# Attention over short sequences: Q and K loaded in 8 KB runs, 32 heads a transfer, with chunks of every other head

## The chip, the cores and the metric

The kernel runs on one core of a Trainium2 chip. The metric is the device time of one execution in microseconds (us), a median over several runs. Profiles come from single executions; their span (first to last instruction) is some 1.8 us shorter than the time measured for the same run.

A core has a matrix engine (TensorE, PE in the profile), a vector engine (VectorE, DVE), a scalar engine (ScalarE, ACT), GpSimd (POOL), a sync engine (SP) and 16 transfer engines (DMA) between HBM and the core's memory (SBUF). Matmuls write to PSUM. Loads issued by GpSimd here also cast fp32 to bf16; their descriptors are made in software ("software_dynamic"). Stores are issued by ScalarE and SP ("hardware_dynamic", queues q10 and q1).

## The reference

```python
batch, n_heads, seq, head_dim = 32, 12, 128, 64       # q, k, v: fp32, randn * 0.1
scores = scale * np.matmul(q, k.transpose(0, 1, 3, 2))  # scale = 1 / sqrt(64)
scores_max = np.max(scores, axis=-1, keepdims=True)
attn = np.exp(scores - scores_max)
attn = attn / (np.sum(attn, axis=-1, keepdims=True) + 1e-8)
return np.matmul(attn, v).astype(np.float32)
```

There are 384 heads of 32 KB a tensor: 37.75 MB are read and 12.58 MB written.

## The kernel before

A chunk is 16 heads in a row, and there are 24. Each partition holds a run of 16 rows of one head (4 KB in HBM). For a chunk, VectorE turns Q and K in blocks of 32 x 32, TensorE computes scores (keys on partitions), ScalarE takes exp, TensorE makes the denominators and the outputs, VectorE turns those back, GpSimd multiplies by the reciprocals, and a store of 512 KB goes out. V comes in 12 blocks of 32 heads and is put in order by matmuls against a permutation ("values").

```python
def runs(x, t):
    return x.rearrange("b h (g t) d -> (b h g) (t d)", t=t).rearrange(
        "(n p) x -> p n x", p=128)

qr, kr, vr, orr = runs(q, TQ), runs(k, TQ), runs(v, T), runs(out, TQ)   # TQ = 16, T = 8

def load_qk(c):                                  # one chunk, 256 KB of bf16 each
    for src, which in ((qr, 0), (kr, 1)):
        x = pin.tile([128, TQ, D], bf16, ...)
        nc.gpsimd.dma_start(out=x, in_=src[:, c, :].rearrange("p (t d) -> p t d", t=TQ))
        chunks[c, which] = x

early = {0: 0, 1: 1, 2: 2, 3: 3, 4: 4, 5: 5}     # which V block is queued behind which chunk's Q and K
early.update({4 * m - 5 + i: 2 * m + i for m in range(3, NCH // 4) for i in range(2)})
# ... (turn, scores, values, denominators, outputs, divide, finish, scale_rows)

def store(c, eng):
    o_sb, _ = osbs.pop(c)
    eng.dma_start(out=orr[:, c, :], in_=o_sb.rearrange("p t d -> p (t d)"))

e = NCH - 1
held = {c: [c - LAG] if c >= LAG else [] for c in range(e - 3)}   # LAG = 9: stores wait nine chunks
held[e - 3] = [e - 12, e - 11, e - 10, e - 9]                     # and go out in bursts at the end
held[e - 2] = [e - 8, e - 7, e - 6]
held[e - 1] = [e - 5, e - 4, e - 3]
held[e] = [e - 2, e - 1, e]
for c in range(NCH):
    todo = shuffles.get(c, [])                   # V block pair c // 4 + 1 is put in order during chunk c
    if c < e:
        turn(c + 1, 0)
        turn(c + 1, 1)
    d_ps = denominators(c)
    if c < e:
        scores(c + 1)
    divide(c, d_ps)
    finish(c, 0, outputs(c, 0))
    # ... values(*x) for the first half of todo, finish(c, 1, outputs(c, 1)), values for the rest
    if c + AHEAD < NCH:                          # AHEAD = 7
        load(c + AHEAD)
    scale_rows(c)
    for s in held[c]:
        store(s, nc.scalar if s < e - 2 else nc.sync)
```

The softmax here doesn't subtract the row's maximum and nothing guards it: scores larger than these inputs give would overflow.

Of the kernel before, what the change touches and what calls it, by code (L numbers as in the profile page):

```python
# [10 lines left out]
def kernel(  # L11
# [8 lines left out]



    nc = tc.nc
    f32 = mybir.dt.float32
    bf16 = mybir.dt.bfloat16

    B, H, S, D = q.shape
    assert S == 128 and D == 64
    scale = 1.0 / (D ** 0.5)
    TQ = 16  # L30
    GQ = S // TQ
    T = 8
    A = 8
    CB = 4
    NCH = B * H // 16
    AHEAD = 7
    LAG = 9

    def runs(x, t):
        return x.rearrange("b h (g t) d -> (b h g) (t d)", t=t).rearrange(  # L40
            "(n p) x -> p n x", p=128)

    qr, kr, vr, orr = runs(q, TQ), runs(k, TQ), runs(v, T), runs(out, TQ)

    singles = ctx.enter_context(tc.tile_pool(name="singles", bufs=1))
    pin = ctx.enter_context(tc.tile_pool(name="pin", bufs=AHEAD + 3))
    pt = ctx.enter_context(tc.tile_pool(name="pt", bufs=3))
    pa = ctx.enter_context(tc.tile_pool(name="pa", bufs=3))
    pf = ctx.enter_context(tc.tile_pool(name="pf", bufs=8))
    po = ctx.enter_context(tc.tile_pool(name="po", bufs=LAG + 3))  # L50
    ps = ctx.enter_context(tc.tile_pool(name="ps", bufs=1, space=bass.MemoryType.PSUM))

    chunks, qts, attns, v2s, osbs = {}, {}, {}, {}, {}

    def load_qk(c):
        for src, which in ((qr, 0), (kr, 1)):
            x = pin.tile([128, TQ, D], bf16, tag="qk"[which] + "_bf", name="qk"[which] + "_bf")
            nc.gpsimd.dma_start(out=x, in_=src[:, c, :].rearrange("p (t d) -> p t d", t=TQ))  # L58
            chunks[c, which] = x

    def load_v(m):

        if m % 2 == 0:
            chunks[m // 2, 2] = pin.tile([128, 2 * CB, T, D], bf16, tag="v_bf", bufs=3, name="v_bf")
        nc.gpsimd.dma_start(  # L65
            out=chunks[m // 2, 2][:, m % 2 * CB:(m % 2 + 1) * CB],
            in_=vr[:, m * CB:(m + 1) * CB, :].rearrange("p n (t d) -> p n t d", t=T))

    with tc.manual_schedule():
        early = {0: 0, 1: 1, 2: 2, 3: 3, 4: 4, 5: 5}  # L70
        early.update({4 * m - 5 + i: 2 * m + i for m in range(3, NCH // 4) for i in range(2)})

        def load(c):
            load_qk(c)
            if c in early:
                load_v(early[c])

        for src, which, eng, cast in ((qr, 0, nc.sync, nc.vector.tensor_copy),
                                      (kr, 1, nc.scalar, nc.scalar.copy)):
            raw = po.tile([128, TQ, D], f32, tag="o_sb", name="raw")  # L80
            eng.dma_start(out=raw, in_=src[:, 0, :].rearrange("p (t d) -> p t d", t=TQ))
            x = pin.tile([128, TQ, D], bf16, tag="qk"[which] + "_bf", name="qk"[which] + "_bf")
            cast(x, raw)  # L83
            chunks[0, which] = x
        load_v(early[0])
        load_qk(1)
        ident = singles.tile([128, 128], bf16)
        make_identity(nc, ident)
        load_v(early[1])
        perm = singles.tile([128, A, 2, 32], bf16)  # L90
        nc.vector.memset(perm, 0.0)
        for tl in range(2):
            nc.vector.tensor_copy(
                perm[:, :, tl, tl * 16:(tl + 1) * 16].rearrange("p a (x g) -> p a x g", x=2),
                ident.rearrange("p (a g x) -> p a x g", a=A, x=2))
        ones = singles.tile([128, 32], bf16)
        nc.vector.memset(ones, 1.0)
        for c in range(2, AHEAD):
            load(c)

        def turn(c, which):


            x = chunks.pop((c, which)).bitcast(f32)
            xt = pt.tile([128, 4, S], f32, tag="qk"[which] + "t", name="qk"[which] + "t")
            if which == 0:
                nc.vector.transpose(xt.rearrange("p h (x g) -> p x h g", g=GQ), x)  # L107
            else:
                nc.vector.transpose(xt.rearrange("p h (x g) -> p x h g", g=GQ),  # L109
                                    x.rearrange("p (y t) e -> p t y e", y=2))  # L110
            qts[c, which] = xt.bitcast(bf16).rearrange("p h (s j) -> p h s j", j=2)

        def scores(c):
            qt, kt = qts.pop((c, 0)), qts.pop((c, 1))
            s_ps = ps.tile([128, 4, 4, S], f32, tag="s_ps", name="s_ps")
            for h in range(4):
                for j in range(2):
                    for b in range(4):
                        pr = slice(b * 32, (b + 1) * 32)
                        nc.tensor.matmul(  # L120
                            s_ps[:, b, h, :], lhsT=kt[pr, h, :, j], rhs=qt[pr, h, :, j],
                            start=(j == 0), stop=(j == 1), tile_position=(b * 32, 0))
            attn = pa.tile([128, 4, 4, S], bf16, tag="attn", name="attn")
            nc.scalar.activation(out=attn, in_=s_ps, func=mybir.ActivationFunctionType.Exp,  # L124
                                 bias=0.0, scale=scale)
            attns[c] = attn

        def values(m, a, heads, half):
# [16 lines left out]
        def denominators(c):  # L145

            d_ps = ps.tile([128, 4, S], f32, tag="w_ps", bufs=4, name="d_ps")
            for b in range(4):
                nc.tensor.matmul(  # L149
                    d_ps[b * 32:(b + 1) * 32], lhsT=ones, rhs=attns[c][:, b],  # L150
                    start=True, stop=True, tile_position=(0, b * 32))
            return d_ps

        def outputs(c, j):

            o_ps = ps.tile([128, 4, S], f32, tag="w_ps", bufs=4, name="o_ps")
            for h in range(4):
                for b in range(4):
                    nc.tensor.matmul(  # L159
                        o_ps[b * 32:(b + 1) * 32, h],  # L160
                        lhsT=v2s[c // 4][:, 4 * (b % 2) + h, 2 * (c % 4) + b // 2,
                                         j * 32:(j + 1) * 32],
                        rhs=attns[c][:, b, h], start=True, stop=True, tile_position=(0, b * 32))
            return o_ps
# [4 lines left out]
        def divide(c, d_ps):  # L169
            dt = pf.tile([128, TQ, 32], f32, tag="dt", name="dt")  # L170
            nc.vector.transpose(dt, turned(d_ps))  # L171
            recip = pf.tile([128, TQ], f32, tag="recip", name="recip")
            nc.vector.reciprocal(recip, dt[:, :, 0])  # L173
            osbs[c] = (po.tile([128, TQ, D], f32, tag="o_sb", name="o_sb"), recip)

        def finish(c, j, o_ps):
            o_sb, _ = osbs[c]
            nc.vector.transpose(o_sb[:, :, j * 32:(j + 1) * 32], turned(o_ps))  # L178

        def scale_rows(c):  # L180
            o_sb, recip = osbs[c]
            if c < NCH - 1:
                nc.gpsimd.tensor_mul(o_sb, o_sb, recip.to_broadcast([128, TQ, D]))  # L183
            else:
                for eng, sl in ((nc.gpsimd, slice(0, 32)), (nc.vector, slice(32, 64))):
                    eng.tensor_mul(o_sb[:, :, sl], o_sb[:, :, sl],  # L186
                                   recip.to_broadcast([128, TQ, 32]))

        def store(c, eng):
            o_sb, _ = osbs.pop(c)  # L190
            eng.dma_start(out=orr[:, c, :], in_=o_sb.rearrange("p t d -> p (t d)"))

        e = NCH - 1
        held = {c: [c - LAG] if c >= LAG else [] for c in range(e - 3)}
# [6 lines left out]
        for c in range(2):  # L201
            shuffles[c] = [(0, 4 * c + 2 * i, 2, 1) for i in range(2)]
            shuffles[c + 2] = [(1, 4 * c + i, 1, None) for i in range(4)]
        turn(0, 0)
        turn(0, 1)
        scores(0)
        for a in range(0, A, 2):
            values(0, a, 2, 0)
        for c in range(NCH):
            todo = shuffles.get(c, [])  # L210
            if c < e:
                turn(c + 1, 0)
                turn(c + 1, 1)
            d_ps = denominators(c)
            if c < e:
                scores(c + 1)
            divide(c, d_ps)
            finish(c, 0, outputs(c, 0))
            for x in todo[:len(todo) // 2]:
                values(*x)  # L220
            finish(c, 1, outputs(c, 1))
            for x in todo[len(todo) // 2:]:
                values(*x)
            if c + AHEAD < NCH:
                load(c + AHEAD)
            scale_rows(c)
            for s in held[c]:
                store(s, nc.scalar if s < e - 2 else nc.sync)
# [30 lines left out]
```

## Time and profile before

| | |
|---|---|
| time, median of 3 runs | 131.39 us (130.83 to 131.76) |
| span of the profiled run | 129.4 us |
| busiest engine | VectorE, 67% |
| transfer engines | at 9 tenths or more in 38 of 40 slices |
| last load lands, last compute ends, last store packet ends | 109.9, 122.5, 127.8 us |

The page's second section cuts the span into 40 slices, a digit for the tenths that an engine was busy. Section 3 has the transfer queues, section 4 the chain of waits followed back from the last instruction, section 5 the groups of instructions (count, busy us, mean ns, then the idle time before them and what ended it). The lines that carry the argument are in the prediction.

### The profile page before, as it was taken

The numbers are of one execution on the slowest core, as the hardware profiler recorded it, in microseconds if no ns is written. First come the engines' busy times: TensorE is split into PE (matmuls) and PEld (weight loads), VectorE is DVE, ScalarE is ACT, GpSimd is POOL, SyncE is SP. The second block draws the span as 40 slices with busy tenths as digits, with TensorE's granted clock in tenths as the row PEclk, the third lists the DMA queues.
The fourth block names the chain that finished last, engine by engine and source line by source line (L and its number), as shares of the span: only waits on it lengthen the run. The fifth ranks groups of instructions, "written<-read, shape, count | busy, mean of one in ns | idle before, by whom it ended". The sixth has DMA issues, their size and how long they took to land.

```text
span 129.4 us, 4637 instructions
## 1 busy us (share of the span) xinstructions
PE 72.9 (56%) x2080; PEld 43.6 (34%) x2080; DVE 86.5 (67%) x150; ACT 71.3 (55%) x74; POOL 79.5 (61%) x88
## 2 busy tenths in 40 slices
PE   0049537597746763886622976460977764856000
PEld 0037335334323442354402454220642442535000
DVE  0246576658879697879944589854578999795800
ACT  3219908567948745865760857580637777335000
POOL 6933133335799986998724895909999445553500
PEclk9999976869999999599996579998555999555555
DMA  3999999999999999999999999999999999999991
GB/s 114 275 193 205 209 209 208 208 210 205 211 208 212 204 211 209 209 208 210 282 288 281 208 212 282 288 286 246 250 209 286 236 298 317 405 414 399 412 408 54
DMA packets 16723, 32.27 MB, mean 249 GB/s; under 512 B 1344, under 2 KB 7488, under 8 KB 16704
## 3 DMA queue, kind: packets, MB, share of 16 engines
q0 software_dynamic: 12960, 18.35, 79.8%
q10 hardware_dynamic: 3168, 11.54, 23.0%
q1 hardware_dynamic: 576, 2.10, 4.2%
q8 instruction: 16, 0.26, 0.7%
q14 instruction: 3, 0.02, 0.0%
HBM read 37.75 MB, written 12.58 MB: 389 GB/s over the span
## 4 chain that ended last, share of the span: by engine, by line
DMA 56%; DVE 14%; POOL 11%; PE 9%; issue 2%; ACT 1%; POOLq 0%; DVEq 0%; ACTq 0%
DMA k_bf<-in_k_dram 34%; DMA q_bf<-in_q_dram 11%; DMA v_bf<-in_v_dram 11%; DVE o_sb L178 6%; PE s_ps L120 5%; POOL o_sb L183 4%; POOL v_bf L65 4%; DVE kt L109 3%; PE o_ps L159 3%; DVE qt L107 3%; POOL q_bf L58 2%; ACT attn L124 1%; PE v_ps L139 1%; DVE o_sb L186 1%; POOL k_bf L58 1%
## 5 line engine op out<-in xcount | busy, mean ns | idle before, releaser
L124 ACT ACTIVATE attn<-s_ps 128x2048 bf16<-128x2048 f32 x24 | 45.1, 1879 | 40.6 <-PE s_ps L120 38.5
L183 POOL TENSOR_TENSOR o_sb<-o_sb,recip 128x1024 f32<-128x1024 f32 x23 | 44.0, 1915 | 9.9 <-DVE o_sb L178 9.7
L178 DVE STREAM_TRANSPOSE o_sb<-o_ps 128x512 f32<-128x512 f32 x48 | 33.3, 712 | 15.7 <-PE o_ps L159 14.8
L120 PE MATMUL s_ps<-qt,kt 32*128 32x128 bf16 x768 | 18.6, 245 | 34.2 <-DVE kt L109 34.2
L139 PE MATMUL v_ps<-v_bf,perm 128*32 128x512 bf16 (+1 forms) x448 | 35.0, 418 | 2.7 <-DMA v_bf<-in_v_dram 2.0
L120 PEld LDWEIGHTS <-kt 32*128 32x128 bf16 x768 | 13.8, 106 | 44.2 <-DVE kt L109 44.2
L143 ACT CAST v<-v_ps 128x512 bf16<-128x512 f32 x48 | 26.1, 593 | 2.1 <-PE v_ps L139 2.0
L159 PE MATMUL o_ps<-attn,v 128*32 128x128 bf16 x768 | 22.9, 251 | 1.1 <-issue 1.0
L58 POOL DMA_DIRECT2D k_bf<-in_k_dram x23 | 12.3, 535 | 15.7 <-DMA v_bf<-in_v_dram 11.6
L109 DVE STREAM_TRANSPOSE kt<-k_bf 128x512 f32<-128x512 f32 x24 | 16.4, 684 | 6.2 <-DMA k_bf<-in_k_dram 6.1
L107 DVE STREAM_TRANSPOSE qt<-q_bf 128x512 f32<-128x512 f32 x24 | 16.3, 679 | 5.5 <-DMA q_bf<-in_q_dram 5.4
L159 PEld LDWEIGHTS <-v 128*32 128x32 bf16 x768 | 16.0, 111 | 10.3 <-issue 5.2
L65 POOL DMA_DIRECT2D v_bf<-in_v_dram x12 | 9.3, 778 | 13.0 <-DMA k_bf<-in_k_dram 4.2
L171 DVE STREAM_TRANSPOSE dt<-d_ps 128x512 f32<-128x512 f32 x24 | 16.3, 680 | 1.0 <-PE d_ps L149 1.0
L149 PE MATMUL d_ps<-attn,ones 128*32 128x512 bf16 x96 | 11.2, 453 | 9.0 <-ACT attn L124 8.9
L58 POOL DMA_DIRECT2D q_bf<-in_q_dram x23 | 13.2, 576 | 3.0 <-DMA k_bf<-in_k_dram 1.3
L139 PEld LDWEIGHTS <-perm 128*32 128x32 bf16 x448 | 11.8, 114 | 6.2 <-issue 3.5
L149 PEld LDWEIGHTS <-ones 128*32 128x32 bf16 x96 | 4.4, 103 | 15.4 <-issue 13.2
L173 DVE RECIPROCAL recip<-dt 128x16 f32<-128x16 f32 x24 | 6.1, 254 | 1.9
L83 DVE CAST q_bf<-raw 128x1024 bf16<-128x1024 f32 x1 | 0.7, 694 | 5.5 <-DMA raw<-in_q_dram 5.5
L83 ACT CAST k_bf<-raw 128x1024 bf16<-128x1024 f32 x1 | 1.0, 1045 | 3.2 <-DMA raw<-in_k_dram 3.2
L83 ACT ACT_TABLE_LOAD x1 | 1.3, 1283 | 1.2 <-PEq L243 1.2
(11 smaller groups left out, 3.9 us busy)
## 6 DMA issues: line engine op xcount, KB each, us to landing
out_dram<-o_sb ACTq DMA_DIRECT2D x21, 512.0 KB, 6.8
v_bf<-in_v_dram POOLq DMA_DIRECT2D x12, 512.0 KB, 13.5
q_bf<-in_q_dram POOLq DMA_DIRECT2D x23, 256.0 KB, 12.4
k_bf<-in_k_dram POOLq DMA_DIRECT2D x23, 256.0 KB, 12.4
out_dram<-o_sb SPq DMA_DIRECT2D x3, 512.0 KB, 6.4
raw<-in_k_dram ACTq DMA_DIRECT2D x1, 512.0 KB, 4.9
raw<-in_q_dram SPq DMA_DIRECT2D x1, 512.0 KB, 4.7
```

Source lines behind the costliest of these rows:

```text
L58: nc.gpsimd.dma_start(out=x, in_=src[:, c, :].rearrange("p (t d) -> p t d", t=TQ))
L107: nc.vector.transpose(xt.rearrange("p h (x g) -> p x h g", g=GQ), x)
L109: nc.vector.transpose(xt.rearrange("p h (x g) -> p x h g", g=GQ), x.rearrange("p (y t) e -> p t y e", y=2))
L120: nc.tensor.matmul(s_ps[:, b, h, :], lhsT=kt[pr, h, :, j], rhs=qt[pr, h, :, j], start=(j == 0), stop=(j == 1), tile_position=(b * 32, 0))
L124: nc.scalar.activation(out=attn, in_=s_ps, func=mybir.ActivationFunctionType.Exp, bias=0.0, scale=scale)
L139: nc.tensor.matmul(v_ps[u * 32:(u + 1) * 32, i], lhsT=perm[:, a + i, tl, :], rhs=v_bf[:, ns, 2 * u + tl, :], start=(tl == 0), stop=(tl == ...
L143: nc.scalar.copy(v2s[m][:, a:a + heads, ns], v_ps)
L149: nc.tensor.matmul(d_ps[b * 32:(b + 1) * 32], lhsT=ones, rhs=attns[c][:, b], start=True, stop=True, tile_position=(0, b * 32))
L159: nc.tensor.matmul(o_ps[b * 32:(b + 1) * 32, h], lhsT=v2s[c // 4][:, 4 * (b % 2) + h, 2 * (c % 4) + b // 2, j * 32:(j + 1) * 32], rhs=attn ...
L171: nc.vector.transpose(dt, turned(d_ps))
L178: nc.vector.transpose(o_sb[:, :, j * 32:(j + 1) * 32], turned(o_ps))
L183: nc.gpsimd.tensor_mul(o_sb, o_sb, recip.to_broadcast([128, TQ, D]))
```

## The change

The intent is longer runs in HBM: 8 KB for Q and K, in half as many transfers. Each partition then holds 32 rows of a head, and 128 partitions hold 32 heads (a duo of chunks). A turn handles all 32 heads, and a chunk takes every other one, so that its output still comes as runs of 16 rows (4 KB). On the HBM side a store is therefore 16 blocks of 8 rows ("16 x 8" or "blocked"): a row here is a run of 4 KB, a block is one head, and between two blocks lies a head of the other chunk. V blocks are queued at every even chunk.

```diff
-    AHEAD = 7
+    NDUO = NCH // 2
+    AHEAD = 5
-    qr, kr, vr, orr = runs(q, TQ), runs(k, TQ), runs(v, T), runs(out, TQ)
+    qr, kr, vr = runs(q, 2 * TQ), runs(k, 2 * TQ), runs(v, T)
+    orr = out.rearrange("b h s d -> (b h s d)").rearrange(
+        "(m k i p x) -> m i k p x", m=NDUO, k=16, i=2, p=8)
...
+    def load_qk(m, which):
+        x = pin.tile([128, 2 * TQ, D], bf16, tag="qk"[which] + "_bf", name="qk"[which] + "_bf")
+        nc.gpsimd.dma_start(
+            out=x, in_=(qr, kr)[which][:, m, :].rearrange("p (t d) -> p t d", d=D))
...
-            xt = pt.tile([128, 4, S], f32, tag="qk"[which] + "t", name="qk"[which] + "t")
+            xt = pt.tile([128, 8, S], f32, tag="qk"[which] + "t", name="qk"[which] + "t")
+            nc.vector.transpose(
+                xt.rearrange("p h (x g) -> p x h g", g=4),
+                x.rearrange("p (y t) e -> p t y e", t=(TQ, T)[which]))
...
-                            s_ps[:, b, h, :], lhsT=kt[pr, h, :, j], rhs=qt[pr, h, :, j],
+                            s_ps[:, b, h, :], lhsT=kt[pr, 2 * h + c % 2, :, j],
+                            rhs=qt[pr, 2 * h + c % 2, :, j],
...
-            nc.scalar.activation(out=attn, in_=s_ps, func=mybir.ActivationFunctionType.Exp,
-                                 bias=0.0, scale=scale)
+            nc.scalar.activation(
+                out=attn.rearrange("p b h (x g y) -> p (b h x) g y", g=4, y=2),
+                in_=s_ps.rearrange("p b h (x y g) -> p (b h x) g y", g=4, y=2),
+                func=mybir.ActivationFunctionType.Exp, bias=0.0, scale=scale)
...
-            eng.dma_start(out=orr[:, c, :], in_=o_sb.rearrange("p t d -> p (t d)"))
+            eng.dma_start(out=orr[c // 2, c % 2], in_=o_sb.rearrange("p t d -> p (t d)"))
...
-            if c < e:
-                turn(c + 1, 0)
-                turn(c + 1, 1)
+            if c < e - 1:
+                turn(c // 2 + 1, c % 2)
...
-            if c + AHEAD < NCH:
-                load(c + AHEAD)
+            if c % 2 == 0 and c // 2 + 6 < NDUO:
+                load_v(c // 2 + 6)
+            if c // 2 + AHEAD < NDUO:
+                load_qk(c // 2 + AHEAD, c % 2)
```

Cut: the buffer counts, the opening loads (1 MB transfers that stay fp32, "raw", for the first duo, cast by halves on VectorE and ScalarE; blocks 2 to 5 of V between the first Q and K), the permutation's pattern, and the head index in the outputs.

More of the change, by code (lines that the diff above doesn't have):

```diff
@@ L41, in runs @@
             "(n p) x -> p n x", p=128)
-    qr, kr, vr, orr = runs(q, TQ), runs(k, TQ), runs(v, T), runs(out, TQ)
+    qr, kr, vr = runs(q, 2 * TQ), runs(k, 2 * TQ), runs(v, T)
+    orr = out.rearrange("b h s d -> (b h s d)").rearrange(
+        "(m k i p x) -> m i k p x", m=NDUO, k=16, i=2, p=8)
     singles = ctx.enter_context(tc.tile_pool(name="singles", bufs=1))
-    pin = ctx.enter_context(tc.tile_pool(name="pin", bufs=AHEAD + 3))
-    pt = ctx.enter_context(tc.tile_pool(name="pt", bufs=3))
+    pin = ctx.enter_context(tc.tile_pool(name="pin", bufs=AHEAD))
+    pt = ctx.enter_context(tc.tile_pool(name="pt", bufs=2))
     pa = ctx.enter_context(tc.tile_pool(name="pa", bufs=3))
@@ L53 @@
     chunks, qts, attns, v2s, osbs = {}, {}, {}, {}, {}
-    def load_qk(c):
-        for src, which in ((qr, 0), (kr, 1)):
-            x = pin.tile([128, TQ, D], bf16, tag="qk"[which] + "_bf", name="qk"[which] + "_bf")
-            nc.gpsimd.dma_start(out=x, in_=src[:, c, :].rearrange("p (t d) -> p t d", t=TQ))
-            chunks[c, which] = x
+    def load_qk(m, which):
+        x = pin.tile([128, 2 * TQ, D], bf16, tag="qk"[which] + "_bf", name="qk"[which] + "_bf")
+        nc.gpsimd.dma_start(
+            out=x, in_=(qr, kr)[which][:, m, :].rearrange("p (t d) -> p t d", d=D))
+        chunks[m, which] = x
     def load_v(m):
@@ L69 @@
     with tc.manual_schedule():
-        early = {0: 0, 1: 1, 2: 2, 3: 3, 4: 4, 5: 5}
-        early.update({4 * m - 5 + i: 2 * m + i for m in range(3, NCH // 4) for i in range(2)})
-        def load(c):
-            load_qk(c)
-            if c in early:
-                load_v(early[c])
-        for src, which, eng, cast in ((qr, 0, nc.sync, nc.vector.tensor_copy),
-                                      (kr, 1, nc.scalar, nc.scalar.copy)):
-            raw = po.tile([128, TQ, D], f32, tag="o_sb", name="raw")
-            eng.dma_start(out=raw, in_=src[:, 0, :].rearrange("p (t d) -> p t d", t=TQ))
-            x = pin.tile([128, TQ, D], bf16, tag="qk"[which] + "_bf", name="qk"[which] + "_bf")
-            cast(x, raw)
-            chunks[0, which] = x
-        load_v(early[0])
-        load_qk(1)
+        for src, which, eng in ((qr, 0, nc.sync), (kr, 1, nc.scalar)):
+            raw = po.tile([128, 2 * TQ, D], f32, tag="raw", bufs=2, name="raw")
+            eng.dma_start(out=raw, in_=src[:, 0, :].rearrange("p (t d) -> p t d", d=D))
+            chunks[0, which] = raw
+        load_v(0)
+        load_qk(1, 0)
         ident = singles.tile([128, 128], bf16)
         make_identity(nc, ident)
-        load_v(early[1])
+        load_qk(1, 1)
+        load_v(1)
         perm = singles.tile([128, A, 2, 32], bf16)
@@ L93, with turn @@
             nc.vector.tensor_copy(
-                perm[:, :, tl, tl * 16:(tl + 1) * 16].rearrange("p a (x g) -> p a x g", x=2),
-                ident.rearrange("p (a g x) -> p a x g", a=A, x=2))
+                perm[:, :, tl, tl * 16:(tl + 1) * 16].rearrange("p a (x g) -> p a x g", x=4),
+                ident.rearrange("p (a g x) -> p a x g", a=A, x=4))
         ones = singles.tile([128, 32], bf16)
         nc.vector.memset(ones, 1.0)
-        for c in range(2, AHEAD):
-            load(c)
-        def turn(c, which):
-            x = chunks.pop((c, which)).bitcast(f32)
-            xt = pt.tile([128, 4, S], f32, tag="qk"[which] + "t", name="qk"[which] + "t")
-            if which == 0:
-                nc.vector.transpose(xt.rearrange("p h (x g) -> p x h g", g=GQ), x)
-            else:
-                nc.vector.transpose(xt.rearrange("p h (x g) -> p x h g", g=GQ),
-                                    x.rearrange("p (y t) e -> p t y e", y=2))
-            qts[c, which] = xt.bitcast(bf16).rearrange("p h (s j) -> p h s j", j=2)
+        for which in range(2):
+            raw = chunks[0, which]
+            x = pin.tile([128, 2 * TQ, D], bf16, tag="qk"[which] + "_bf", name="qk"[which] + "_bf")
+            nc.vector.tensor_copy(x[:, :TQ], raw[:, :TQ])
+            nc.scalar.copy(x[:, TQ:], raw[:, TQ:])
+            chunks[0, which] = x
+        for m in range(2, AHEAD):
+            if m == 3:
+                load_v(3)
+            load_qk(m, 0)
+            load_qk(m, 1)
+            if m == 2:
+                load_v(2)
+            if m == 3:
+                load_v(4)
+                load_v(5)
+        def turn(m, which):
+            x = chunks.pop((m, which)).bitcast(f32)
+            xt = pt.tile([128, 8, S], f32, tag="qk"[which] + "t", name="qk"[which] + "t")
+            nc.vector.transpose(
+                xt.rearrange("p h (x g) -> p x h g", g=4),
+                x.rearrange("p (y t) e -> p t y e", t=(TQ, T)[which]))
+            qts[m, which] = xt.bitcast(bf16).rearrange("p h (s j) -> p h s j", j=2)
         def scores(c):
-            qt, kt = qts.pop((c, 0)), qts.pop((c, 1))
+            qt, kt = qts[c // 2, 0], qts[c // 2, 1]
             s_ps = ps.tile([128, 4, 4, S], f32, tag="s_ps", name="s_ps")
@@ L160, in outputs @@
                         o_ps[b * 32:(b + 1) * 32, h],
-                        lhsT=v2s[c // 4][:, 4 * (b % 2) + h, 2 * (c % 4) + b // 2,
+                        lhsT=v2s[c // 4][:, 2 * h + c % 2, 4 * (c // 2 % 2) + b,
                                          j * 32:(j + 1) * 32],
```

## The prediction

> **What bounds the kernel now.** I read the page from section 2 down. The rows of busy tenths come first, because they tell whether one resource is full in every stage or each stage has its own limit.
>
> ```profile
> DVE  0246576658879697879944589854578999795800
> ACT  3219908567948745865760857580637777335000
> PEclk9999976869999999599996579998555999555555
> DMA  3999999999999999999999999999999999999991
> GB/s 114 275 193 205 209 209 208 208 210 205 211 208 212 204 211 209 209 208 210 282 288 281 208 212 282 288 286 246 250 209 286 236 298 317 405 414 399 412 408 54
> ```
>
> Each digit is a slice of 3.2 us. No engine is full throughout (VectorE 67%, the others less), but the transfer engines are, from the second slice to the last but one. The GB/s row counts a casting transfer (fp32 in HBM, bf16 in SBUF) by what it writes: 208 there is 416 GB/s read. Pure loads (416) and pure stores (399 to 414, right end) thus move the same bytes per second. The queues and the HBM totals confirm it:
>
> ```profile
> q0 software_dynamic: 12960, 18.35, 79.8%
> q10 hardware_dynamic: 3168, 11.54, 23.0%
> q1 hardware_dynamic: 576, 2.10, 4.2%
> HBM read 37.75 MB, written 12.58 MB: 389 GB/s over the span
> ```
>
> 50.33 MB at 413 GB/s is 121.9 us of a span of 129.4. In the packet records the first transfer of data starts at 1.75 us and the last ends at 127.6. The 125.85 us between are the 121.9 plus dips: about 0.8 us of ramp before 2.9, 0.8 between 4.9 and 7.7, 0.4 near 108.7 where loads end, and 1.1 at the end, where some engines finish first.
>
> The chain of waits agrees: up to 89.8 us it runs through loads, then through compute.
>
> ```profile
> DMA 56%; DVE 14%; POOL 11%; PE 9%; issue 2%; ACT 1%; POOLq 0%; DVEq 0%; ACTq 0%
> 73.47 16.28 DMA k_bf<-in_k_dram
> ...
> 121.38 1.10 DVE L186 TENSOR_TENSOR o_sb<-o_sb,recip 128x512 f32<-128x512 f32 x1
> ```
>
> The last line, from the timeline, is the last compute: it ends at 122.5. The backlog of stores then still needs 5 us (0.5 MB at 413 GB/s is 1.27 us, so about three stores remained besides their landing). **So transfers set the end, and compute has some 2.5 us of slack there**; a gain in compute alone would buy nothing.
>
> **What the Trainium skill says.** (1) "DMA: Bandwidth & Descriptors", section "Where 436 GB/s comes from": a ceiling of 435 GB/s for the 16 engines, so 27.2 bytes per ns each and 150.6 ns for 4 KB. The trace agrees: 413 to 417 when full. (2) Same page, "Why small descriptors are slow (HBM only)": about 3 cycles lost per packet; at the 850 MHz named there I estimate 3.5 ns. I checked this on the packet records: for each us from 8 to 107 I counted packets of each kind and solved by least squares for the engine time of each: 79.0 ns for a V packet (2 KB read), 154.9 for a Q or K packet (4 KB), 16.4 for the 4-byte completion packet, 162 for a 4 KB store. A straight line through the first two is 3.1 ns plus 75.9 per 2 KB. (The durations recorded, 98 and 173 ns, overlap and are not occupancy.) (3) "ScalarE: Activation LUTs", "What ACT_TABLE_LOAD costs": 186 ns + 0.833 ns per element with immediate scale and bias, 1892 for 2048 elements; the trace has 1879. (4) "SBUF — State Buffer", "Door 1: The DMA port swizzle", notes lines of 8 bytes in PSUM and a cost where accesses cross lines. No instruction of the kernel before reads PSUM on ScalarE with a stride, so this trace can't say.
>
> **The change part by part.**
>
> ```profile
> L124 ACT ACTIVATE attn<-s_ps 128x2048 bf16<-128x2048 f32 x24 | 45.1, 1879 | 40.6 <-PE s_ps L120 38.5
> L109 DVE STREAM_TRANSPOSE kt<-k_bf 128x512 f32<-128x512 f32 x24 | 16.4, 684 | 6.2 <-DMA k_bf<-in_k_dram 6.1
> L107 DVE STREAM_TRANSPOSE qt<-q_bf 128x512 f32<-128x512 f32 x24 | 16.3, 679 | 5.5 <-DMA q_bf<-in_q_dram 5.4
> L83 DVE CAST q_bf<-raw 128x1024 bf16<-128x1024 f32 x1 | 0.7, 694 | 5.5 <-DMA raw<-in_q_dram 5.5
> ```
>
> 1. Packets of Q and K, on the bounding resource. Before: 46 casting transfers of 128 packets, 5888 x 154.9 = 912 us of engine time, and 256 raw packets x 159 = 41. After: 22 transfers, 2816 packets of 8 KB at 3.1 + 4 x 75.9 = 306.7, 864 us, and 256 raw at about 310, 79. Saved: 10 us over 16 engines, **0.6 us**.
> 2. Completion packets: 16 for each transfer, 736 to 352; 384 x 16.4 / 16 = **0.4 us**.
> 3. Start. The dip from 4.9 to 7.7 us lies where the 1 MB of raw loads has run out and the first casting V load runs alone at 220 to 380 GB/s. With 2 MB of raw loads (5.1 us from about 2.4) that stretch is filled: **0.8 us**.
> 4. Stores keep 4 KB runs and 512 KB each: nothing.
> 5. VectorE: one turn of 1024 elements a chunk for two of 512. Two take 1.19 us start to start in the tail (114.05 to 115.24); one should take 1.15 to 1.2. Nothing. But scores of an odd chunk need no turn of their own any more, which shortens the compute loop (3.64 us when TensorE's clock is full, 4.2 to 4.9 when it is at half) by a few tenths. Off the bound.
> 6. GpSimd issues 24 fewer transfers at 0.55 us: off the bound.
> 7. First compute: raw lands near 8 us instead of 5.5, then four half casts (694 ns VectorE, 1045 ScalarE) and two turns of 1.2: scores start near 12 us, not 8.2. It costs nothing if later chunks are held by loads, which they are: V block 3 lands near 28 us, before and after.
> 8. Exp now reads PSUM in pairs 16 bytes apart. I take its time as unchanged.
>
> End of compute: K of the last 32 heads lands about 2.4 + 36 x 2.54 us of loads + 11 stores of 1.27 = 108; three chunks follow, 11 to 12 us, so compute ends near 120 and stores stay in backlog. Sum: 131.39 - 0.6 - 0.4 - 0.8 = **129.6 us**.
>
> **Rivals.** (a) The strided PSUM read slows exp. At twice the time, ScalarE needs 3.7 + 1.1 (two V copies) + 0.3 per chunk, 5.1 us, as much as the 5.1 us of transfers (2.1 MB); the three last chunks each take 1.3 us longer, the slack is used up, and the time would be 133 to 136. For: the skill's note. Against: VectorE turns PSUM with strides (L178, 48 times 712 ns) about as fast as SBUF (679), though there in runs of 32 bytes. One in seven. (b) Stores whose HBM side is now 16 blocks of 8 rows spread worse over the engines: 5% on 12.6 MB is 1.5 us, time 131. (c) Larger packets gain more than the line says. The bound is the ceiling itself: (154.9 - 150.6) x 5888 / 16 = 1.6 us at most, time 128.6. (d) Coarser loads: compute waits for 32 heads at a time, so at the end it comes late and transfers starve. Against: the last load is issued three chunks earlier, and eight transfers in flight are now always about 8 MB. It would cost 1 to 2 us, time 131.
>
> **Range and chances.** 129.6 is 1.4% less, so within 2% is likeliest. Faster by over 2% (under 128.8) needs (c) or the dips at 108.7 and the end to go too: 0.17. Slower by over 2% needs (a): 0.13. The range is 128.0 to 132.8, skewed for (a), (b) and (d).
>
> **What would show it.** Right: the transfers' row still at 9 throughout, packets of 4 KB written on the software queue, loads at 208 to 212 from the third slice, exp at 1.88 us, last compute near 120. Wrong: exp above 2.2 us; a GB/s row below 400 in the last slices (starved); stores over 170 ns a packet; turns well over 1.2 us.

## The result

| | before | changed |
|---|---|---|
| time, median of 4 runs | 131.13 us (130.83 to 131.76) | 136.13 us (135.47 to 136.75) |
| span of the profiled run | 129.4 us | 133.7 us |
| last load lands | 109.9 us | 106.5 us |
| last compute ends | 122.5 us | 124.3 us |
| last packet of a store ends | 127.8 us | 132.1 us |

The ratio is 1.0374, with a 95% interval of 1.0302 to 1.0447: **slower**, by 3.7%. A ratio is the mean time of one kernel's fast runs over that of the other's in the same rounds, so it isn't quite the ratio of the medians.

The page of the changed kernel, its rows of busy tenths and GB/s and its software queue, which answer to those of before:

```profile
DVE  0137359902897966998983869870099899547100
...
DMA  3999999999999999999999999999999959999991
GB/s 93 410 237 217 205 219 205 207 218 206 206 221 203 215 213 209 214 203 218 252 309 236 272 261 230 281 281 290 214 216 271 319 136 273 375 342 348 386 354 48
...
q0 software_dynamic: 9504, 17.83, 71.5%
```

The loads go as fast as before. The last eight slices don't: 136 and 273 where the last loads end, then 342 to 386 where the kernel before had 399 to 414. VectorE has a hole of two slices before that (00, 90 to 97 us). The page's own digit for DMA hides most of it, since a packet that is slow still counts as busy. So I weighed each packet of the records by what a packet of its kind takes when the engines are full (fitted anew, by the prediction's method, which had 154.9 and 162 where I have 154.6 and 159.5; in ns: V 79, 4 KB of Q or K 154.6, 8 KB 305.2, store 159.5, raw 8 KB 310 by the same line, completion 16.4), summed that over each stretch, and divided by 16. (Other ways to fit the same records give 79 to 81, 155 to 159, 304 to 306 and 165 to 176, so a few tenths of a us below mean nothing.) What is lacking from the stretch's length is lost:

| us | before | changed |
|---|---|---|
| transfer work in the whole run | 122.6 | 121.4 |
| lost from 0 to 12 us | 3.2 | 3.3 |
| 12 to 103 | 0.5 | 0.4 |
| 103 to 108 | 0.0 | 1.0 |
| 108 to 114 | 0.4 | 2.8 |
| from 114 to the end | 2.7 | 4.8 |

The work fell by 1.2 us (roughly: 1 ns more or less for each of the 5,888 packets of 4 KB is 0.4 us), but 5.4 us more were lost after 103 us. These lines say what the compute engines did. The groups of the changed kernel:

```profile
L133 ACT ACTIVATE attn<-s_ps 128x2048 bf16<-128x2048 f32 x24 | 45.0, 1877 | 25.0 <-PE s_ps L128 19.7
...
L150 PE MATMUL v_ps<-v_bf,perm 128*32 128x512 bf16 (+1 forms) x448 | 34.7, 411 | 16.2 <-DMA v_bf<-in_v_dram 15.3
...
L116 DVE STREAM_TRANSPOSE qt<-q_bf 128x1024 f32<-128x1024 f32 x12 | 14.5, 1212 | 1.8 <-DMA q_bf<-in_q_dram 1.8
...
L116 DVE STREAM_TRANSPOSE kt<-k_bf 128x1024 f32<-128x1024 f32 x12 | 14.4, 1202 | 0.0
```

The same matmuls of V in the kernel before:

```profile
L139 PE MATMUL v_ps<-v_bf,perm 128*32 128x512 bf16 (+1 forms) x448 | 35.0, 418 | 2.7 <-DMA v_bf<-in_v_dram 2.0
```

Exp and the turns cost what was expected. New are the 15.3 us (2.0 before) for which TensorE waited for V. The timeline of the changed kernel shows the longest of these waits (start, duration, instruction, and in brackets the idle time before it):

```profile
65.33 0.81 POOL L70 DMA_DIRECT2D v_bf<-in_v_dram  x1
...
88.99 0.65 DVE L189 STREAM_TRANSPOSE o_sb<-o_ps 128x512 f32<-128x512 f32 x1
...
95.22 1.04 PE L150 MATMUL v_ps<-v_bf,perm 128*32 128x512 bf16 x8 [7.18 <-DMA v_bf<-in_v_dram]
...
109.45 4.08 ACTq L202 DMA_DIRECT2D out_dram<-o_sb  x4
```

The last V block is issued at 65.33 and lands at 95.2. It is needed in chunk 16, which stands still for 7.2 us. In the kernel before, the last V block was issued later, at 69.80, and TensorE never waited over 0.8 us for V. The difference is the time that V lies in the queue, first before and then changed:

```profile
DMA to landing us min/median/max: 7.6/13.5/17.9
```

```profile
DMA to landing us min/median/max: 10.1/20.7/29.8
```

The 29.8 us are the last block's. The transfer engines are full all that time, so nothing is lost yet. But the chunks behind it, and the stores that hang on them, come late. When the loads end at 106.5 there is one store queued at a time; the first burst of four goes out at 109.45.

The stores themselves changed too. Their issues in the kernel before (min, median, max ns):

```profile
L191 ACTq DMA_DIRECT2D out_dram<-o_sb x21: 338/339/1212, 57.9 to 118.1; - x21
```

and in the changed kernel:

```profile
L202 ACTq DMA_DIRECT2D out_dram<-o_sb x21: 546/564/2159, 61.3 to 122.7; - x21
```

In the packet records, a store's packet that starts after 110 us, when stores run alone, took 162.5 ns on average before, with 1% of them over 200 ns. In the changed kernel it is 185.7, with 16% over 200. Between 60 and 100 us, among loads, both have 172.

So there were two suspects. **Theory A**: V stands too far back in the queue of loads. **Theory B**: the stores with a 16 x 8 HBM side are slow. A rival to both, **theory C**, is that loads of 32 heads are simply too coarse.

### The profile page after: what moved, and what is told of

The parts are those of the page before. It is cut to its first block, busy times and chain, and to the rows that moved or that the text cites. A ratio compares the mean times of both kernels' runs of the same rounds, so it can differ in the third digit from the quotient of the medians.

```text
span 133.7 us, 4590 instructions
## 1 busy us (share of the span) xinstructions
PE 71.1 (53%) x2080; PEld 42.9 (32%) x2080; DVE 82.8 (62%) x127; ACT 72.7 (54%) x75; POOL 67.1 (50%) x64
## 4 chain that ended last, share of the span: by engine, by line
DMA 66%; DVE 7%; POOL 7%; PE 5%; ACT 4%; issue 3%; ACTq 1%; DVEq 0%; POOLq 0%
DMA v_bf<-in_v_dram 38%; DMA k_bf<-in_k_dram 25%; ACT attn L133 4%; POOL o_sb L194 4%; DVE o_sb L189 3%; DMA out_dram<-o_sb 3%; PE s_ps L128 2%; PE d_ps L160 2%; POOL q_bf L62 1%; ACTq L202 1%; DVE dt L182 1%; DVE kt L116 1%; DVE qt L116 1%; DVE o_sb L197 1%; PE v_ps L150 1%
## 5 line engine op out<-in xcount | busy, mean ns | idle before, releaser
L133 ACT ACTIVATE attn<-s_ps 128x2048 bf16<-128x2048 f32 x24 | 45.0, 1877 | 25.0 <-PE s_ps L128 19.7
L189 DVE STREAM_TRANSPOSE o_sb<-o_ps 128x512 f32<-128x512 f32 x48 | 32.5, 695 | 23.9 <-PE o_ps L170 23.4
L150 PE MATMUL v_ps<-v_bf,perm 128*32 128x512 bf16 (+1 forms) x448 | 34.7, 411 | 16.2 <-DMA v_bf<-in_v_dram 15.3
L128 PE MATMUL s_ps<-qt,kt 32*128 32x128 bf16 x768 | 17.8, 237 | 22.1 <-DVE kt L116 22.1
L170 PE MATMUL o_ps<-attn,v 128*32 128x128 bf16 x768 | 22.3, 243 | 1.5 <-issue 1.4
L128 PEld LDWEIGHTS <-kt 32*128 32x128 bf16 x768 | 13.1, 102 | 31.0 <-DVE kt L116 27.0
L182 DVE STREAM_TRANSPOSE dt<-d_ps 128x512 f32<-128x512 f32 x24 | 16.4, 683 | 5.7 <-PE d_ps L160 5.5
L116 DVE STREAM_TRANSPOSE qt<-q_bf 128x1024 f32<-128x1024 f32 x12 | 14.5, 1212 | 1.8 <-DMA q_bf<-in_q_dram 1.8
L62 POOL DMA_DIRECT2D q_bf<-in_q_dram x11 | 5.9, 541 | 18.1 <-DMA v_bf<-in_v_dram 7.6
L116 DVE STREAM_TRANSPOSE kt<-k_bf 128x1024 f32<-128x1024 f32 x12 | 14.4, 1202 | 0.0
L62 POOL DMA_DIRECT2D k_bf<-in_k_dram x11 | 6.4, 577 | 7.5 <-DMA v_bf<-in_v_dram 2.8
L97 ACT CAST q_bf<-raw 128x1024 bf16<-128x1024 f32 x1 | 1.0, 1045 | 6.5 <-DMA raw<-in_q_dram 6.5
## 6 DMA issues: line engine op xcount, KB each, us to landing
v_bf<-in_v_dram POOLq DMA_DIRECT2D x12, 512.0 KB, 20.7
```

The source lines that it names most:

```text
L62: nc.gpsimd.dma_start(out=x, in_=(qr, kr)[which][:, m, :].rearrange("p (t d) -> p t d", d=D))
L116: nc.vector.transpose(xt.rearrange("p h (x g) -> p x h g", g=4), x.rearrange("p (y t) e -> p t y e", t=(TQ, T)[which]))
L128: nc.tensor.matmul(s_ps[:, b, h, :], lhsT=kt[pr, 2 * h + c % 2, :, j], rhs=qt[pr, 2 * h + c % 2, :, j], start=(j == 0), stop=(j == 1), til ...
L133: nc.scalar.activation(out=attn.rearrange("p b h (x g y) -> p (b h x) g y", g=4, y=2), in_=s_ps.rearrange("p b h (x y g) -> p (b h x) g y" ...
L150: nc.tensor.matmul(v_ps[u * 32:(u + 1) * 32, i], lhsT=perm[:, a + i, tl, :], rhs=v_bf[:, ns, 2 * u + tl, :], start=(tl == 0), stop=(tl == ...
L170: nc.tensor.matmul(o_ps[b * 32:(b + 1) * 32, h], lhsT=v2s[c // 4][:, 2 * h + c % 2, 4 * (c // 2 % 2) + b, j * 32:(j + 1) * 32], rhs=attns[ ...
```

## The experiments

All are edits of the changed kernel, unless said otherwise. Only e1, e8 and e10 give a correct result. The others give a wrong one, since only where a store goes is changed; they compute and move as much as the others. The waits for V below are totals of TensorE's matmuls for them. "Slow" runs among these (1.5% above the fastest of the same kernel, on a single core) are left out of the ratios. The kernels with blocked stores have more of them: 5 of the 16 runs of the changed kernel, e1, e2 and e8, against 1 of 25 with plain or strided stores (e10 aside). So for e1, e2 and e8 the ratio may be on the low side, and the medians, over all runs, lie higher.

| run | edit | median us | ratio to before (95%) | lost 103 to 114 us | lost from 114 |
|---|---|---|---|---|---|
| changed | | 136.13 | 1.0374 (1.0302 to 1.0447) | 3.8 | 4.8 |
| e1 | V first | 134.18 | 1.0223 (1.0170 to 1.0276) | (slow) | (slow) |
| e2 | before, blocked stores | 133.61 | 1.0118 (1.0059 to 1.0177) | (slow) | (slow) |
| e3 | plain stores | 132.42 | 1.0102 (1.0053 to 1.0151) | 2.5 | 3.2 |
| e4 | V first, plain stores | 130.88 | 1.0007 (0.9938 to 1.0075) | 1.1 | 2.9 |
| e6 | rows 8 KB apart | 132.70 | 1.0061 (0.9970 to 1.0152) | 2.2 | 3.5 |
| e7 | e4, early tail | 130.79 | 0.9950 (0.9877 to 1.0024) | 0.2 | 2.8 |
| e8 | e1, early tail, opening order | 134.73 | 1.0163 (1.0062 to 1.0264) | 1.0 | 5.4 |
| e9 | e8, plain stores | 130.67 | 0.9929 (0.9859 to 0.9999) | 1.0 | 3.0 |
| e10 | half queries | 163.74 | 1.2321 (1.2174 to 1.2467) | | |
| e11 | early tail, plain stores | 132.19 | 1.0066 (0.9987 to 1.0145) | 3.2 | 3.0 |

The losses are those of the profiled run, weighed as above; "(slow)" marks profiled runs of the slow state, which I don't read for this. There is no run e5 on record.

### e1: V first

```diff
-            if c % 2 == 0 and c // 2 + 6 < NDUO:
-                load_v(c // 2 + 6)
+            if c % 4 < 2 and c // 4 < 3:
+                load_v(6 + c // 4 * 2 + c % 4)
```

> The changed kernel with V blocks 7, 9 and 11 queued ahead of the K (32 heads) they now stand behind; nothing else. Theory A (the order of the loads: TensorE waited 15.3 us for V, 7.2 of it at chunk 16, stores came late, and the transfer engines were starved from 104 to 114 us, about 4 us of them lost): the waits for V fall under 9 us, the one of 7.2 goes, GB/s stays near 400 where loads end, and the time falls by 3 to 4.5 us, to 132 to 133. Theory B (the stores with a 16 x 8 HBM side are slow by themselves): the waits go but the time falls by under 1.5 us. Theory C (coarse loads of 32 heads): nothing much.

The median is 134.18 us, the fast runs 133.44 to 134.20. The ratio fell by 1.5%, about 2 us, its interval clear of the changed kernel's. Both expectations missed: theory A wanted 3 to 4.5 us, theory B under 1.5. Theory A also wanted the waits for V under 9 us and the long one gone. In this run's profile (a slow one) they are 11.6 us, the longest 6.3. The order is part of the cause and not all of it.

### e2: the kernel before with blocked stores

```diff
-    qr, kr, vr, orr = runs(q, TQ), runs(k, TQ), runs(v, T), runs(out, TQ)
+    qr, kr, vr = runs(q, TQ), runs(k, TQ), runs(v, T)
+    orr = out.rearrange("b h s d -> (b h s d)").rearrange(
+        "(m k i p x) -> m i k p x", m=NCH // 2, k=16, i=2, p=8)
-            eng.dma_start(out=orr[:, c, :], ...)
+            eng.dma_start(out=orr[c // 2, c % 2], ...)
```

> The kernel before, with only the HBM side of its stores taken from the changed one (16 blocks of 8 rows; the result is wrong on purpose, heads land in each other's places). Theory A: at most 1 us slower. Theory B: stores in the last 18 us take more than 175 ns a packet instead of 162, some over 300, and the time rises by 2 to 4 us, to 133 to 135.

The median is 133.61 us (2.7 over before), the fast runs 132.37 and 132.76. Kernels are compared only within the same rounds. Nothing else was changed, so the store's shape alone slows the kernel before too: by 1.2%, some 1.5 us, by the two fast runs, and by 2.0% by the medians of all runs. By the fast runs that is less than the 2 to 4 us of theory B and more than the 1 us that theory A allowed. Its profile is of a slow run, but shows what the fast ones of the changed kernel and of e8 show (16 and 14%): 13.4% of the store packets after 110 us took over 200 ns.

### e3: the changed kernel with plain stores

```diff
-    orr = out.rearrange("b h s d -> (b h s d)").rearrange(
-        "(m k i p x) -> m i k p x", m=NDUO, k=16, i=2, p=8)
+    orr = runs(out, TQ)
-            eng.dma_start(out=orr[c // 2, c % 2], in_=o_sb.rearrange("p t d -> p (t d)"))
+            eng.dma_start(out=orr[:, c, :], in_=o_sb.rearrange("p t d -> p (t d)"))
```

> The changed kernel with the stores of the one before (128 rows, one block; the result is wrong on purpose). Theory A: under 1 us faster. Theory B: 2 to 4 us faster, 132 to 134, packets of the last slices back at 160 to 165 ns.

132.42 us, so 3.7 us of the median and 2.7% of the ratio are gone, within theory B's range. Store packets after 110 us are back at 164.5 ns, 0.8% over 200. TensorE still waits 16.7 us for V, which leaves theory A for what remains over the kernel before; e4 tests it.

### e4: both

> Both edits at once (result wrong on purpose). If A and B are both in it and nothing else is, the time is what the prediction had, 129 to 130.5. If a third cause is in it (C), it stays over 132.

130.88 us, a ratio of 1.0007. Both causes are real and nearly add up: 1.5% and 2.7% alone, 3.7% together. The last slices of this kernel's GB/s row are those of the kernel before again:

```profile
GB/s 101 409 249 211 202 219 213 197 214 211 202 215 213 203 211 213 217 210 208 214 293 280 274 247 262 251 298 265 264 212 242 261 307 301 403 407 401 407 408 37
```

The last compute ends at 121.8, not 124.3. Still, the expectation was 129 to 130.5: the profile had lost 1.1 us where loads end. So a third cause of the size that theory C needs (over 132) is ruled out, but a smaller one is not. For the waits for V only shrank:

```profile
PE v_ps L149 <- DMA v_bf<-in_v_dram: 11.6, 5, 5.3
```

(total, times, longest; 15.3, 5, 7.2 in the changed kernel.) Chunk 16 goes on at 92.9 instead of 95.1 (e3), since the last V block still lies 30.0 us in the queue. No run here has shorter loads or fewer of them ahead, so what that queue costs stays open.

### e6: gaps without blocks

```diff
-        "(m k i p x) -> m i k p x", m=NDUO, k=16, i=2, p=8)
+        "(m p i x) -> m i p x", m=NDUO, p=128, i=2)
```

> The changed kernel, its stores with gaps in HBM as now, but as 128 rows of 4 KB each 8 KB from the next, so that the HBM side is 128 rows again and not 16 blocks of 8 (result wrong on purpose). If the slow stores come from how 16 x 8 is dealt out to the transfer engines: as fast as with plain stores, 131.7 to 133, tail packets at 160 to 166 ns, issue on ScalarE 0.34 us. If they come from the gaps in HBM: slow as the changed kernel, 135 to 137, tail packets at 175 to 190 ns.

132.70 us: with e3, not with the changed kernel. The stores' issues in this kernel:

```profile
L202 ACTq DMA_DIRECT2D out_dram<-o_sb x21: 338/339/1802, 61.3 to 119.0; - x21
```

Issue is back at 339 ns and packets after 110 us at 164.6 (0.8% over 200 ns). Gaps in HBM cost nothing, at this spacing at least. It's the 16 x 8 shape of the HBM side that makes an issue longer and the packets slow.

### e7 and e11: stores released earlier at the end

```diff
-        held[e - 3] = [e - 12, e - 11, e - 10, e - 9]
-        held[e - 2] = [e - 8, e - 7, e - 6]
-        held[e - 1] = [e - 5, e - 4, e - 3]
+        held[e - 4] = [e - 13, e - 12, e - 11]
+        held[e - 3] = [e - 10, e - 9, e - 8]
+        held[e - 2] = [e - 7, e - 6, e - 5]
+        held[e - 1] = [e - 4, e - 3]
```

> V first and plain stores (result wrong on purpose), and the stores of chunks 11 and on released one iteration earlier, so that a burst is queued when the loads end at 107 us. If the 0.9 us that the transfer engines still lacked work from 103 to 108 is what is left of the gap to the prediction: 129.6 to 130.3, and that idle under 0.4 us. If it's something else: 130.5 to 131.5, no change.

> The changed kernel with plain stores (result wrong on purpose) and the early tail, but V in its late place. If late V costs only because stores are held when the loads end, releasing them earlier does what V first did: 130.5 to 131.2, idle from 103 to 114 us under 0.7 (it was 2.5). If late V costs by itself, as late chunks at the end: 131.5 to 132.5.

In e7 (V first) the loss between 103 and 114 us went from 1.1 to 0.2 us in the profiled run, the fastest of its five, but the median moved by 0.1 us only, and the ratio from 1.0007 to 0.9950, with intervals that overlap: the release isn't worth more than the noise. In e11 (V late) it doesn't replace V first: 132.19 us, as e3 without it. So late V costs by itself: the last compute ends at 124.8 in e11 and at 121.9 in e7. The intervals of these two ratios just overlap, but all three pairs that differ in V alone (e1, e4 and e7 against the changed kernel, e3 and e11) go the same way, by 1.5, 1.0 and 1.2%.

### e8 and e9: all orders, with blocked and with plain stores

```diff
             load_qk(m, 0)
+            if m < 4:
+                load_v(2 * m - 2)
+                load_v(2 * m - 1)
             load_qk(m, 1)
-            if m == 2:
-                load_v(2)
...
```

> The changed kernel, correct: V blocks first, in the opening loads too (blocks 2 to 5 ahead of the K that is needed later), and the early tail. Stores stay in 16 x 8. Waits for V under 5 us. If order was all of theory A, 132 to 133.5; the slow stores keep it above the kernel before.

> The same with plain stores (result wrong on purpose): all found causes out. 129 to 130 if the prediction's sum of transfer work (1.0 us less than before) was right and nothing else is in the way; the opening orders should be worth under 0.5 us, since the transfer engines are full there in any order.

e8 is correct and was to be the best the changed layout can do: 134.73 us (fast runs 133.31 and 133.94), above the 132 to 133.5 expected and no better than e1 beyond noise, and its wait for V stayed at 10.5 us against the 5 expected. e9 has 130.67 us where 129 to 130 was expected, 0.7% under the kernel before with an interval that ends at 0.9999, but a wrong result. The opening order was worth nothing that these runs can tell (e9 against e7).

### e10: half the queries of all heads

e6's rows can be had with a correct result if a chunk is half the queries of all 32 heads instead of all queries of half of them.

```diff
-            for h in range(4):
+            qs = slice(c % 2 * 64, c % 2 * 64 + 64)
+            for h in range(8):
...
-                            s_ps[:, b, h, :], lhsT=kt[pr, 2 * h + c % 2, :, j],
-                            rhs=qt[pr, 2 * h + c % 2, :, j],
+                            s_ps[:, b, h, :], lhsT=kt[pr, h, :, j],
+                            rhs=qt[pr, h, qs, j],
...   (outputs alike; Q turned in plain order, exp in plain order; V first, early tail, e6's store)
```

> A correct kernel that keeps the 8 KB loads and has the plain store spread: a chunk is half the queries of all 32 heads, so its output is 128 rows of 4 KB, 8 KB apart (the shape that ran fast as rows_8k_apart); V first and early tail too. Price: 128 matmuls of 64 columns a chunk for scores and outputs in place of 64 of 128 columns, at some 20 to 25 ns each about 1 to 1.5 us more of TensorE a chunk. If transfers still set the end: correct, 130 to 131, at most 1% under the kernel before. If the tail becomes TensorE's: 132 to 135, with transfer engines idle over 1 us between 108 and 120 us.

Correct, but 163.74 us, far off both forecasts. I had priced the extra matmuls by their own durations. The waits of this kernel show another bill (the profile is of a run 1.7% above the fastest; the excess is 23%):

```profile
PEld L129 <- issue: 29.6, 25, 3.2
...
PE s_ps L129 <- issue: 20.3, 12, 3.1
PEld L169 <- issue: 14.3, 24, 4.5
```

TensorE stands still for 2 to 4 us at a time, most often before score matmuls, waiting for nothing that these lines show. The queue of instructions says more:

```profile
q8 instruction: 28, 0.46, 1.1%
```

It moved 28 packets of 16 KB for 7,232 matmuls and weight loads, and 16 for 4,160 in the changed kernel: one for about 256. In the records, TensorE has 12 gaps of 1.9 to 4.4 us between 20 and 115 us that no semaphore explains. They lie 255 or 256 of its instructions apart, or a multiple of that, and at 11 of them such a packet starts within 0.8 us of the gap's start (2.1 us after it at the twelfth). Together they are 31 us; the span is 33 us longer than e9's. So the stalls lie where TensorE's next block of instructions is fetched. That is read from one trace: no run tests it, and why the fetch came late here, and not in the changed kernel, stays open.

## Why the prediction was wrong

**What held.** The bound was named rightly: transfers set the end, and every microsecond lost by them after 103 us shows in the time. Steps 1 and 2 held in size, as far as the fit can tell: 8 KB packets take 305.2 ns by the same fit (306.7 predicted), and the transfer work fell by about 1.2 us (1.0 predicted). The price of a packet in the Trainium skill, "DMA: Bandwidth & Descriptors", "Why small descriptors are slow (HBM only)", about 3 cycles (3.5 ns, an estimate at the page's 850 MHz), agrees with the 3.1 ns of the prediction's fit. Step 5 held, with 1.2 us a turn. Step 8 held, and rival (a), the one I gave most weight, fell: exp is 1877 ns with its PSUM reads 16 bytes apart.

**The step that failed first: "Stores keep 4 KB runs and 512 KB each: nothing."** The run length stayed, but how a store is dealt out did not. By e3 against the changed kernel and e4 against e1 it cost 2.7 and 2.2%, 3.7 and 3.3 us of the medians; in the kernel before (e2) 1.2%. I had it as rival (b) with an estimate of 5% on all stores, 1.5 us, and left it out of the sum. Measured, it isn't 5% on all stores: among loads no difference shows (172 ns a packet), alone it is 14% (185.7 against 162.5), plus 0.22 us an issue. That e2 cost some 1.5 us too fits the estimate's size, not its reason. An estimate from the records: 1,739 packets after 110 us, 23 ns more each, over 16 engines, are 2.5 us, the larger part of what it cost here; slower packets and longer issues weren't tested apart. Why 16 x 8 is slow wasn't measured either. The Trainium skill, "DMA: Bandwidth & Descriptors", "The descriptor swizzle", says that a 128-partition transfer gives each engine two groups of four partitions on one port of SBUF; "SBUF — State Buffer", "Door 1: The DMA port swizzle", has partitions 0 to 3 on one port and 4 to 7 on another. If 16 blocks of 8 rows go one block to an engine, engines share ports, and packets may now and then wait for each other. That is a guess and isn't shown: the records here don't tell engines apart, and it doesn't say why stores among loads look the same.

**The step that failed second: "K of the last 32 heads lands about ... 108; three chunks follow".** The sum counted K alone. V had been checked for block 3 in the opening (step 7) and for no later one. The same count for the last V block, 32nd in the queue, gives 2.4 + 32 x 2.54 + 8 stores x 1.27 = 94; it landed at 95.2, and chunk 16 wanted it at 88. K itself landed in time (the loads end at 106.5), but compute stood further back by then and ended 17.8 us later, not 11 to 12. By e4 against e3 and e1 against the changed kernel this cost 1.0 and 1.5%, 1.5 and 2.0 us of the medians. Rival (d), "compute comes late and transfers starve", is what happened, and its 1 to 2 us were the right size, though for V and not for the 32 heads of K that it named. With three V blocks each put ahead of one transfer of K (e4 against e3), the loads as coarse as ever, chunk 16 went on 2.2 us sooner and the starving fell from 2.5 to 1.1 us. Its argument against, that loads are issued earlier, didn't help V: the last block was issued 4.5 us earlier than before and lay 29.8 us in the queue, behind Q and K prefetched ten chunks deep. The prediction had the number for this: eight transfers in flight of 1 MB each are 8.4 MB, 20 us at its 413 GB/s, and Q, K and V took 20.0 to 20.7 us from issue to landing (medians; 12.4 to 13.5 before).

**The third, small one: step 3.** The dip from 4.9 to 7.7 us was partly filled (lost from 4 to 12 us: 0.8 before, 0.5 after), but the first 4 us lost 2.8 instead of 2.4. In sum the 0.8 us were not gained. (The prediction's account of the span has a slip too, which its sum doesn't use: 121.9 and its dips add up to 125.0, not 125.85, and 127.6 us is where the last data packet starts; it ends at 127.8.)

With all this out (e7, e9) the time is 130.7 to 130.8, 0.5 to 0.7% under the kernel before (e7's interval still holds 1); the prediction minus its step 3 would be 130.4. Its chances of 0.13 for slower were too low, since they rested on exp alone. No correct kernel beats the one before.

## What to carry to other kernels

When transfers are the bound, list every stream that goes through the queue with the place at which it is issued and the chunk that needs it, and check each one's deadline to the end, not just the opening's. A store is described by the shape of both its sides, not only by its run length: look at a store stream where it runs alone, and at the spread of packet times rather than at the busy share. Prefetching one stream deeper pushes back every stream behind it in the same queue.

## What the Trainium skill lacked or had wrong

- "DMA: Bandwidth & Descriptors", "Why a DMA increments its semaphore by 16 and not by 1": it says how many engines a transfer of a given shape uses, not what a shape costs whose two sides are split differently. Measured, with 128 partitions on one side and 16 blocks of 8 rows on the other: 185.7 ns a 4 KB packet in a stretch of stores alone, 16% of them over 200, against 162.5 and 1% for 128 rows; 0.56 us to issue instead of 0.34; 172 ns both ways among loads.
- "SBUF — State Buffer", "Door 1: The DMA port swizzle": its note on PSUM lines of 8 bytes names matmuls and doesn't say whether ScalarE pays. Reading 2048 fp32 values from PSUM in pairs 16 bytes apart took 1877 ns here, 1879 in order.
- "Runtime: NRT & Kernel Launch", "Instruction fetch mechanics": it has instructions refilled in blocks of 16 KiB, 256 instructions, and calls the cost of crossing into the next block mostly hidden. The size agrees (28 packets for 7,232 matmuls and weight loads in e10). The cost was not hidden there: 12 gaps of 1.9 to 4.4 us at such places, 31 us in all, by one trace. In the changed kernel, with 4,160, the matmuls' waits that nothing explains are 2.0 us in all.
